# Moving a kernel's tiles by a few bytes: slots shifted by 96 bytes, and a different offset for each buffer of the weight ring

## The chip, the cores and the metric

The kernel runs on one core of a Trainium2 chip. The metric is device time of one execution in microseconds (us). Three plain executions of the kernel before took 3236.25, 3236.37 and 3238.22 us; their median is 3236.37 us.

## The reference

Two kinds of transformer block, each twice, on one sequence of 512 positions with 1024 channels, in float32. What matters here is that almost all arithmetic is products of activations with weights:

```python
for l in range(2):                       # first block
    h = rmsnorm(x, norm_mix_pre[l])
    proj = h @ w_in[l]                   # 1024 -> 7168, split into ten parts
    ...                                  # retention, two depthwise convolutions
    merged = gates0 * (ret @ w_ret_out[l]) + gates1 * (sc @ w_sc_out[l]) + gates2 * (cf @ w_cf_out[l])
    x = x + rmsnorm(merged @ w_o[l], norm_mix_post[l])
    h = rmsnorm(x, norm_ffn_pre[l])
    up = causal_dwconv(h @ w_up[l], ffn_conv_w[l])          # 1024 -> 2 * 2816
    x = x + rmsnorm((silu(gate) * val) @ w_down[l], norm_ffn_post[l])
for l in range(2):                       # second block
    proj = rmsnorm(x, pre_norm_g_2[l]) @ w_in_2[l]          # 1024 -> 10432, twelve parts
    ...                                  # gated MLP over positions, attention, a linear recurrence
    x = x + rmsnorm(merged @ w_out_2[l], post_norm_g_2[l])
```

## The kernel before

Every product is done three times over, because each float32 operand is kept as two float32r tiles, a rounded one (hi) and the rest (lo): `mm3` (lines 322, 323, 324) issues hi·hi, hi·lo and lo·hi, each with 128 rows and mostly 512 columns. A product on TensorE has a stationary operand, which a weight load brings in first, and a moving operand, which streams past it. In a row of the trace `p<-hh,whi` the name after the arrow is the moving operand and the last name the stationary one.

The operands live in four places.
- `hh` and `hl` hold the normalised activations h, transposed, hi and lo: 8 slices of 512 columns each.
- The weight ring: `wp` has seven buffers `whi` and seven `wlo`, each of 1024 columns. Weights stream from memory in pairs of pieces (`raw`, two buffers). `Stream._split` turns piece c into `whi` on ScalarE (line 179) and `wlo` on VectorE (line 180), some four pieces ahead of TensorE. Piece c lies in the buffer of c modulo 7, and there are 544 pieces.
- 48 slots `s0` to `s47` of 512 columns hold everything else: other activations (each as a hi and a lo slot when a product needs them), gates, gains. A slot that is released goes to the end of the list of free ones, and the next request takes the first of the list.
- `raw`, the small tiles and constants.

So there are three kinds of products by where the operands lie. In `projT` with h the ring is stationary and h moves (in `tok_proj` and `mla_down` the other way round). In `projT` with another operand the ring is stationary and slots move. In `out_proj` slots are stationary and the ring moves. Retention and attention multiply slots by slots.

The pools stand in a partition's memory one behind the other, in the order in which they are opened: fixed tiles, the ring, `raw`, the small tiles, the slots. Each ring buffer has 4096 bytes per partition and each slot 2048. In the built program `hh`, `hl`, all 14 ring buffers and `raw` begin 96 bytes past a multiple of 128 bytes, and all slots begin at a multiple of 128. All slices that the products take from them start a multiple of 256 bytes further on. So where h meets the ring, both operands have the same place within 128 bytes, and where a slot meets the ring, they stand 96 bytes apart.

Of the kernel before, what the change touches and what calls it, by code (L numbers as in the profile page):

```python
# [8 lines left out]
F32 = mybir.dt.float32  # L9
F32R = mybir.dt.float32r  # L10
# [13 lines left out]
RING = 7  # L24
AHEAD = 4
RAW = 2
NSLOT = 48


C_Q, C_K, C_V, C_G = 0, 256, 512, 1024  # L30
# [79 lines left out]
class Slots:  # L110
    def __init__(self, pool, n, tag):
        self.pool, self.tag = pool, tag
        self.free_ = deque(range(n))
        self.where = {}
        self.low = n
        self.cnt = 0
# [30 lines left out]
class Stream:  # L147
# [21 lines left out]
    def _split(self, c):  # L169
        nc = self.k.nc  # L170
        p = c // 2
        while self.loaded <= p:
            self._load(self.loaded)
            self.loaded += 1
        raw = self.raw[p]
        src = raw[:, 1024 * (c % 2):1024 * (c % 2) + 1024]
        hi = self.k.wp.tile([128, 1024], F32R, tag="whi", name=f"whi{c}")
        lo = self.k.wp.tile([128, 1024], F32R, tag="wlo", name=f"wlo{c}")
        nc.scalar.activation(hi[:], src, AF.Copy)  # L179
        nc.vector.tensor_tensor(lo[:], src, hi[:].bitcast(F32), op=ALU.subtract)  # L180
        self.parts[c] = (hi, lo)
        self.parts.pop(c - RING, None)

        if c % 2 == 1 and self.total is not None:
            if self.loaded < (self.total + 1) // 2 and self.loaded <= p + RAW:
                self._load(self.loaded)
                self.loaded += 1
# [50 lines left out]
class Kernel:  # L238
    def __init__(self, nc, tc, ctx, aps, total):
        self.nc, self.tc = nc, tc  # L240
        self.x_in, self.w, self.pv_in, self.rows, self.gmw, self.cst, self.out = aps
        fixed = ctx.enter_context(tc.tile_pool(name="fixed", bufs=1))
        self.wp = ctx.enter_context(tc.tile_pool(name="wp", bufs=RING))
        self.rawp = ctx.enter_context(tc.tile_pool(name="rawp", bufs=RAW))
        self.sm = ctx.enter_context(tc.tile_pool(name="small", bufs=6))
        self.s = Slots(ctx.enter_context(tc.tile_pool(name="slots", bufs=1)), NSLOT, "s")
        self.p = Slots(ctx.enter_context(tc.tile_pool(name="psum", bufs=1, space=bass.MemoryType.PSUM)), 8, "p")
        self.ws = Stream(self, total)
        self.ident = fixed.tile([128, 128], F32, tag="ident", name="ident")
        self.pv = fixed.tile([128, PV["n"]], F32, tag="pv", name="pv")  # L250
        self.half = fixed.tile([128, 4], F32, tag="half", name="half")
        self.hh = fixed.tile([128, KD, S], F32R, tag="hh", name="hh")
        self.hl = fixed.tile([128, KD, S], F32R, tag="hl", name="hl")
        self.xd = tc.dram_tile((S, D), F32, name="xd")
        self.h_op = [Op(self.hh[:, k, :], self.hl[:, k, :]) for k in range(KD)]
        self.lanes = {}
        self.x_src = self.x_in
        self.pend = None
        self.ht = {}
        self.pre = {}  # L260
        self.x = {}
# [1243 lines left out]
```

## Time and profile before

| | |
|---|---|
| median of three executions | 3236.37 us |
| profiled execution, whole time | 3238.38 us |
| its span, first to last instruction | 3236.5 us |
| TensorE busy | 3181.7 us (98%), 14808 matmuls |
| weight loads busy | 2650.7 us (82%) |
| VectorE, ScalarE, GpSimd busy | 58%, 37%, 8% |
| mean share of the 2.4 GHz TensorE clock granted | 0.994 |

The 1.9 us by which the whole time exceeds the span lie before and behind the first and last instruction. Matmuls are pipelined: the next one starts while one still shows as busy, so a matmul's duration in a row is longer than its share of the time. What a matmul costs is the step from its start to the start of the next one.

### The profile page before, as it was taken

To read this page: it belongs to the slowest core of one execution; us is meant where nothing else is said; L and a number is where in the kernel's file an instruction comes from. 1 tells how busy PE (TensorE), PEld (TensorE's weight loads), DVE (VectorE), ACT (ScalarE), POOL (GpSimd) and SP (SyncE) were. 2 spreads that over 40 slices of the span, in tenths; PEclk is the share of its full clock that TensorE was granted. 3 is DMA by queue.
4 is the path that set the end of the run, shared out by engine and by line. 5 is a ranking of instruction groups with operands and counts; after the bars stand their busy time and mean duration, and the time that the engine had idled before them with its cause. 6 is when DMAs were issued, how large, how long until landed. Compare 5 with 4: busy or idle time off the path is not lost. (4 is left out here: it accounts for less than half of the span.)

```text
span 3236.5 us, 36908 instructions
## 1 busy us (share of the span) xinstructions
PE 3181.7 (98%) x14808; PEld 2650.7 (82%) x14808; DVE 1867.2 (58%) x2729; ACT 1191.5 (37%) x1798; POOL 255.9 (8%) x362
## 2 busy tenths in 40 slices
PE   8999999999999999999999999999999999999998
PEld 7888888888888888888888887788888888778886
DVE  5687556663568755666358536635446844663643
ACT  4222343332422234333345526512234543632222
POOL 2000010000200001000010002200002001210000
PEclk9999999999999999999999999999999999999999
DMA  5222322232422232223222224322333213332221
GB/s 194 92 97 91 130 90 93 101 113 102 153 92 98 91 130 79 104 93 115 104 104 93 78 95 125 112 104 91 108 121 124 78 67 120 98 124 104 91 104 72
DMA packets 62540, 337.98 MB, mean 104 GB/s; under 512 B 10305, under 2 KB 10433, under 8 KB 27553
## 3 DMA queue, kind: packets, MB, share of 16 engines
q1 hardware_dynamic: 49984, 302.54, 26.5%
q0 software_dynamic: 11232, 31.08, 3.3%
q8 instruction: 116, 1.90, 0.2%
q10 hardware_dynamic: 1152, 2.01, 0.2%
q14 instruction: 56, 0.45, 0.0%
HBM read 310.68 MB, written 8.39 MB: 99 GB/s over the span
## 5 line engine op out<-in xcount | busy, mean ns | idle before, releaser
L322 PE MATMUL p<-hh,whi 128*128 128x512 f32 (+1 forms) x2752 | 1052.7, 383 | 1.6 <-ACT whi L179 1.6
L324 PE MATMUL p<-hh,wlo 128*128 128x512 f32 (+1 forms) x2752 | 1048.6, 381 | 1.5 <-DVE wlo L180 1.5
L323 PE MATMUL p<-hl,whi 128*128 128x512 f32 (+1 forms) x2752 | 1048.4, 381 | 0.0
L180 DVE TENSOR_TENSOR wlo<-raw,whi 128x1024 fp32r<-128x1024 f32 x544 | 675.7, 1249 | 522.0 <-ACT whi L179 520.8
L179 ACT ACTIVATE whi<-raw 128x1024 fp32r<-128x1024 f32 x544 | 562.7, 1052 | 287.8 <-PE p L324 197.6
L322 PEld LDWEIGHTS p<-hh,whi 128*128 128x128 f32 x2752 | 521.0, 189 | 99.6 <-ACT whi L179 2.0
L324 PEld LDWEIGHTS p<-hh,wlo 128*128 128x128 f32 x2752 | 520.0, 189 | 100.5 <-DVE wlo L180 1.8
L323 PEld LDWEIGHTS p<-hl,whi 128*128 128x128 f32 x2752 | 520.5, 189 | 96.8
L323 PE MATMUL p<-s,whi 128*128 128x512 f32 (+1 forms) x768 | 306.1, 399 | 2.4 <-POOL s L307 2.4
L322 PE MATMUL p<-s,whi 128*128 128x512 f32 (+1 forms) x768 | 305.9, 398 | 1.8 <-ACT s L306 1.8
L324 PE MATMUL p<-s,wlo 128*128 128x512 f32 (+1 forms) x768 | 305.7, 398 | 0.0
L323 PE MATMUL p<-wlo,s 128*128 128x512 f32 x640 | 254.1, 397 | 0.0
L322 PE MATMUL p<-whi,s 128*128 128x512 f32 x640 | 253.7, 396 | 0.0
L324 PE MATMUL p<-whi,s 128*128 128x512 f32 x640 | 252.3, 394 | 0.0
L306 ACT ACTIVATE s<-s 128x512 fp32r<-128x512 f32 x168 | 103.2, 627 | 363.6 <-DVE s L688 133.7
L672 ACT ACTIVATE s<-p 128x512 f32<-128x512 f32 x96 | 57.3, 597 | 468.6 <-PE p L324 468.6
L812 DVE SCALAR_TENSOR_TENSOR s<-p,pv,s 128x511 f32<-128x511 f32 (+1 forms) x176 | 131.8, 749 | 122.3 <-ACT s L809 119.2
L683 DVE TENSOR_TENSOR s<-p,s 128x512 f32<-128x512 f32 x96 | 66.3, 691 | 203.6 <-PE p L324 203.5
L566 DVE SCALAR_TENSOR_TENSOR s<-s,pv,s 128x511 f32<-128x511 f32 (+14 forms) x240 | 176.1, 734 | 5.7
L323 PEld LDWEIGHTS p<-s,whi 128*128 128x128 f32 (+1 forms) x768 | 145.5, 189 | 37.8 <-POOL s L307 3.9
L322 PEld LDWEIGHTS p<-s,whi 128*128 128x128 f32 (+1 forms) x768 | 145.0, 189 | 35.8 <-ACT s L306 2.7
L324 PEld LDWEIGHTS p<-s,wlo 128*128 128x128 f32 (+1 forms) x768 | 145.5, 189 | 34.5
(187 smaller groups left out, 3077.5 us busy)
## 6 DMA issues: line engine op xcount, KB each, us to landing
raw<-in_w_dram SPq DMA_DIRECT2D x272, 1024.0 KB, 4.8
s<-in_rows_dram POOLq DMA_DIRECT2D x32, 256.0 KB, 3.5
s<-s POOLq DMA_DIRECT2D x96, 64.0 KB, 2.5
xd<-s SPq DMA_DIRECT2D x24, 256.0 KB, 2.0
s<-xd POOLq DMA_DIRECT2D x24, 256.0 KB, 3.3
s<-s SPq DMA_DIRECT2D x88, 64.0 KB, 2.7
s<-in_cst_dram POOLq DMA_DIRECT2D x16, 256.0 KB, 3.8
s<-in_x_dram POOLq DMA_DIRECT2D x8, 256.0 KB, 5.8
```

The source lines that it names most:

```text
L179: nc.scalar.activation(hi[:], src, AF.Copy)
L180: nc.vector.tensor_tensor(lo[:], src, hi[:].bitcast(F32), op=ALU.subtract)
L306: self.nc.scalar.activation(hi[:, :n], t[:, :n], AF.Copy)
L322: mm(ps, a[0], b[0], start=first, stop=False)
L323: mm(ps, a[0], b[1], start=False, stop=False)
L324: mm(ps, a[1], b[0], start=False, stop=last)
L566: nc.vector.scalar_tensor_tensor(c[:, sh:], glu[:, :S - sh], w(k), c[:, sh:], op0=ALU.mult, op1=ALU.add)
L672: nc.scalar.activation(sgs[m][:], pg[:], AF.Sigmoid)
L683: nc.vector.tensor_tensor(sg[:], py[:], sg[:], op=ALU.mult)
L812: nc.vector.scalar_tensor_tensor(t[:, sh:], ps[:, :S - sh], w(k), t[:, sh:], op0=ALU.mult, op1=ALU.add)
```

## The change

```diff
-NSLOT = 48
+NSLOT = 47
+
+HI_AT = (0, 8, 16, 24, 4, 12, 20)
+LO_AT = (28, 2, 6, 10, 14, 18, 30)
...
-        hi = self.k.wp.tile([128, 1024], F32R, tag="whi", name=f"whi{c}")
-        lo = self.k.wp.tile([128, 1024], F32R, tag="wlo", name=f"wlo{c}")
+        hi = self.k.wp.tile([128, 1024 + 32], F32R, tag="whi", name=f"whi{c}")
+        lo = self.k.wp.tile([128, 1024 + 32], F32R, tag="wlo", name=f"wlo{c}")
+        ho, lo_ = HI_AT[c % RING], LO_AT[c % RING]
+        hi, lo = hi[:, ho:ho + 1024], lo[:, lo_:lo_ + 1024]
         nc.scalar.activation(hi[:], src, AF.Copy)
         nc.vector.tensor_tensor(lo[:], src, hi[:].bitcast(F32), op=ALU.subtract)
...
         self.sm = ctx.enter_context(tc.tile_pool(name="small", bufs=6))
+        self.sm.tile([128, 24], F32, tag="shift", name="shift", bufs=1)
```

A ring buffer grows from 4096 to 4224 bytes, 33 times 128, so all buffers still begin 96 bytes past a multiple of 128; the piece in it begins a further 0 to 120 bytes on. In bytes, by c modulo 7, `whi` is moved by 0, 32, 64, 96, 16, 48, 80 and `wlo` by 112, 8, 24, 40, 56, 72, 120. The tile `shift` of 96 bytes, which nothing reads or writes, stands ahead of the slots, and with it the 47 slots begin 96 bytes past a multiple of 128, as `hh` and `hl` do. The 14 times 128 bytes take the room of one slot.

So after the change h and the slots have one place within 128 bytes, and the distance from either of them to the ring is the offset of the piece. No engine's instructions are moved, added or left out: on each of the five engines the built programs have the same rows in the same order, but for the numbers of slots.

## Rows read from the trace of the kernel before

**Rows 1.** The page: span, busy time of TensorE, granted clock in 40 slices.
```profile
span 3236.5 us, 36908 instructions
PE 3181.7 (98%) x14808; PEld 2650.7 (82%) x14808; DVE 1867.2 (58%) x2729; ACT 1191.5 (37%) x1798; POOL 255.9 (8%) x362
PEclk9999999999999999999999999999999999999999
```

**Rows 2.** Matmuls by line and shape: count | busy us, mean ns | idle before, releaser.
```profile
L322 PE MATMUL p<-hh,whi 128*128 128x512 f32 x2496 | 978.1, 392 | 0.0
L324 PE MATMUL p<-hh,wlo 128*128 128x512 f32 x2496 | 974.9, 391 | 0.0
L323 PE MATMUL p<-s,whi 128*128 128x512 f32 x752 | 299.7, 399 | 2.4 <-POOL s L307 2.4
L323 PE MATMUL p<-wlo,s 128*128 128x512 f32 x640 | 254.1, 397 | 0.0
L323 PE MATMUL p<-wlo,hh 128*128 128x512 f32 x192 | 74.8, 390 | 0.0
L322 PE MATMUL p<-hh,whi 128*128 128x256 f32 x256 | 74.6, 291 | 1.6 <-ACT whi L179 1.6
L324 PE MATMUL p<-hh,wlo 128*128 128x256 f32 x256 | 73.8, 288 | 1.5 <-DVE wlo L180 1.5
L323 PE MATMUL p<-wlo,hh 128*128 128x384 f32 x64 | 23.2, 362 | 5.1 <-DVE wlo L180 5.1
L1170 PE MATMUL p<-s,whi 96*128 96x512 f32 x24 | 10.7, 446 | 10.5 <-DVE whi L1160 10.5
L323 PE MATMUL p<-s,whi 112*128 112x512 f32 x16 | 6.4, 401 | 0.0
L999 PE MATMUL p<-s,s 128*128 128x512 f32 x16 | 6.3, 397 | 0.0
L1000 PE MATMUL p<-s,s 128*128 128x512 f32 x16 | 6.3, 392 | 0.0
```

**Rows 3.** Timeline of TensorE, h moving, ring stationary: start us, us, instruction.
```profile
199.75 0.39 PE L323 MATMUL p<-hl,whi 128*128 128x512 f32 x1
...
208.59 0.39 PE L323 MATMUL p<-hl,whi 128*128 128x512 f32 x1
```

**Rows 4.** The same, halves of h (256 columns) moving.
```profile
1280.91 0.28 PE L323 MATMUL p<-hl,whi 128*128 128x256 f32 x1
...
1282.95 0.28 PE L322 MATMUL p<-hh,whi 128*128 128x256 f32 x1
```

**Rows 5.** The same, ring moving, slots stationary.
```profile
446.20 0.40 PE L322 MATMUL p<-whi,s 128*128 128x512 f32 x1
...
453.20 0.40 PE L322 MATMUL p<-whi,s 128*128 128x512 f32 x1
```

**Rows 6.** The same, slots moving, then h, the ring stationary in both.
```profile
1913.69 0.40 PE L322 MATMUL p<-s,whi 128*128 128x512 f32 x1
...
1920.02 0.39 PE L322 MATMUL p<-hh,whi 128*128 128x512 f32 x1
...
1922.11 0.39 PE L322 MATMUL p<-hh,whi 128*128 128x512 f32 x1
...
1923.92 0.39 PE L324 MATMUL p<-hh,wlo 128*128 128x512 f32 x1
```

**Rows 7.** What TensorE waited for: us in total, times, longest us.
```profile
PE p L415 <- DVE s L399: 15.6, 8, 10.9
PE p L1170 <- DVE whi L1160: 10.5, 2, 5.3
PE p L323 <- DVE wlo L180: 5.1, 4, 1.8
...
PE p L1026 <- DVE s L1015: 2.4, 2, 1.2
```

**Rows 8.** The two instructions that fill the ring.
```profile
L180 DVE TENSOR_TENSOR wlo<-raw,whi 128x1024 fp32r<-128x1024 f32 x544 | 675.7, 1249 | 522.0 <-ACT whi L179 520.8
L179 ACT ACTIVATE whi<-raw 128x1024 fp32r<-128x1024 f32 x544 | 562.7, 1052 | 287.8 <-PE p L324 197.6 <-DMA raw<-in_w_dram 67.4 <-DVE wlo L180 9.1
```

## The prediction

> **What bounds the kernel now.** I read the page first: TensorE is busy for 98% of the span and its clock is granted in full in all 40 slices [rows 1]. Then the list of its waits: the three longest kinds come to 31 us of 3236, and those for the ring's two fillers are a few us [rows 7]. So nothing feeds TensorE late; the kernel takes as long as its matmuls stand one behind the other. The next question is what one matmul costs, as the step from start to start, and that is read from timelines.
>
> Where h meets the ring, 39 steps of 512-column matmuls take 208.59 - 199.75 = 8.84 us, 226.7 ns each [rows 3]. Halves of 256 columns take (1282.95 - 1280.91) / 17 = 120.0 ns [rows 4]. The 256 further columns thus cost 106.7 ns, 0.417 ns each, which is one column per period of 2.4 GHz. So 512 columns are 213.3 ns, and each matmul carries 13.3 ns on top.
>
> Where a slot meets the ring, the same matmul costs more: 7.00 us for 30 steps, 233.3 ns, with the ring moving and slots stationary [rows 5]; 6.33 us for 27, 234.4 ns, with slots moving and the ring stationary [rows 6]. The groups by shape show that this holds over the span: mean durations of 390 to 392 ns with h against 397 to 399 with slots, in either role [rows 2]. Shape, lines and clock are the same; what differs is where the operands lie. With h both stand at the same place within 128 bytes, with a slot they are 96 bytes apart. That is no proof: slots are another region too, and they are written by more engines. One stretch helps. When h takes over from slots, the first 9 steps still take 2.09 us, 232.2 ns each, and only then do 8 steps take 1.81 us, 226 ns [rows 6]. So an equal place does not give the short step at once; a run of like matmuls settles into it. And slot against slot, at equal places (both at 0) but in chains of a few matmuls, shows 392 and 397 ns [rows 2], like unsettled ones.
>
> **The change part by part.** The matmuls that it touches are counted from the groups. With h: 3 x 2496 + 3 x 192 = 8064 of 512 columns, now at 226.7 ns. With slots against the ring: 3 x 752 + 3 x 640 = 4176, and 72 more of the recurrence's gates (3 x 16 of 112 rows and 24 of 96), 4248, now at 233.9 ns (the mean of 233.3 and 234.4 by their counts). Both kinds will meet the ring under the same conditions, since h and slots come to one place; call their common step x. The time changes by 8064 (x - 226.7) + 4248 (x - 233.9) ns, which is nothing at x = 229.2 ns.
>
> What is x? The step is set by the moving operand of one matmul and the weights that are loaded beside it for the next one. Two of three loads with a stationary ring are `whi`, one is `wlo`. Of the seven `whi` places one has offset 0, as h has now: between 226.7 ns settled and 232.2 unsettled, I take 229.5. Two have 32 and 96 bytes, which are the two distances (96 bytes in one direction or the other, counted within 128) that slots have now: 233.9 ns. The other four, and all `wlo`, have distances that the trace does not show. Their bounds are the nearest rows on either side, 226.7 and 233.9; between them I take the middle, 230.3. Below 226.7 no settled stretch goes, though 213.3 ns of columns is the floor. Then x = 2/3 (229.5 + 2 x 233.9 + 4 x 230.3) / 7 + 1/3 x 230.3 = 2/3 x 231.2 + 76.8 = 230.9 ns. With h that is +4.2 ns x 8064 = +33.9 us, with slots -3.0 ns x 4248 = -12.7 us, together +21 us.
>
> The Trainium skill speaks against counting anything here ("SBUF — State Buffer", section "Who interferes with whom"): TensorE has two independent read ports, one for the moving operand and one for weight loads, and never waits on anyone. By it the step would not depend on places and the sum would be nothing. The trace doesn't bear that out as it stands: equal shapes differ by 7 ns.
>
> The 256-column matmuls (768), the 384- and 320-column ones (384) and slot against slot: the first have 13.3 ns on top as the long ones do, and by the same 4.2 ns could add up to 5 us; slot against slot keeps equal places. I put 2 us down for the lot. The ring's fillers: 1052 and 1249 ns for a piece [rows 8], each once in 3236 / 544 = 5.9 us, four pieces ahead. Written at other offsets they may get longer, but VectorE is busy for 58% and a tenth more on 1249 ns stays within the idle time ahead of it (522 us in all, for the ring's other filler). If that cover were gone, TensorE's waits for the two, now 8 us [rows 2, 7], would grow; I put nothing. One slot fewer: the free list of 48 was down to one left at 4 of 1538 requests, all in attention; with 47 it is empty there, and 14 requests find one or none behind them. Each then waits for the last reader of a slot just released, and behind it wait the split or copy on that engine and the scores' matmuls. TensorE's longest kind of wait in attention is 2.4 us now [rows 7]; between nothing and some 5 us, I take 1.
>
> Sum: 21 + 2 + 1 = +24 us on 3238.4 us, the profiled execution's own time, which is 2 us above the median of the runs. On the median that gives 3236.4 + 24 = 3260 us.
>
> **The rivals.**
> *All steps as bad as slots now.* If any distance but 0 gives 233.9 ns, and pieces change too often to settle, x = 233.9: 8064 x 7.2 = +58 us, 3294 us. For it: only distance 0, in long runs, shows the short step. Against it: only two other distances are known.
>
> *The other side: faster.* If settling needs only that distances stay put within a piece (24 matmuls with one pair of buffers), and slots lose what made them slow, x = 226.7: -7.2 x 4248 = -31 us, 3206 us. It decides from x below 229.2 ns on. For it: an unsettled stretch lasts 9 steps and a piece has 24. Against it: with slots, whose distance is the same in every matmul, long stretches never settle [rows 5, 6].
>
> *No change.* If the 7 ns belong to the slots' region and not to the place within 128 bytes, x stays at either value, 3236 us. For it: slot against slot is slow at equal places. Against it: the unsettled stretch has h alone and is nearly as slow, 232.2 ns.
>
> *Far faster.* If distances exist at which a load and a stream don't meet at all, the 13.3 and 20 ns on top shrink. Halving both would give -6.7 x 8064 - 10.3 x 4248 = -98 us, 3139 us. No row shows any such step. The Trainium skill has a rule for it ("TensorE: Matmul & The Clock Gate", section "Back-to-back issue gap"): a warm matmul's gap is N / 2.4 + 2.5 ns, 216 ns at 512 columns; by it, as an estimate, the kernel would come to 3236 - 8064 x 0.0107 - 4248 x 0.0179 = 3074 us. The trace shows 226.7 at best.
>
> **How the numbers follow.** A measurement of this kernel can tell about 0.2%, 6.5 us, from no change. Mixed steps, x from 229.8 to 232.8 (+8 to +45 us): 0.45; the forecast, 3260 us, with a range of its own of 3244 to 3281. All bad, beyond +45: 0.14. No change within 6.5 us, by place or by balance: 0.13. Settled steps, faster by up to 45 us: 0.24. Far faster: 0.04. So faster 0.28, same 0.13, slower 0.59. The range reaches from the settled case, 3206, to just under the worst, 3292.
>
> **What would show it.** In the groups by shape the 512-column durations with h should rise from 391 to about 395 ns, and those with slots should fall from 398 to about the same. Timelines should show steps that differ from piece to piece with a period of seven pieces: shortest where c modulo 7 is 0, some 234 ns at 1 and 3. TensorE's waits, the fillers' means and attention should stay as they are. The prediction is wrong if h keeps 391 ns, if slots keep 398, or if the new distances give steps under 226 ns.

## The result, and the profile after

The changed kernel takes 3256.34 us (median of three executions, 3253.68 to 3256.89) against 3236.37 us: 1.0062 times as long, with a 95% interval of 1.0044 to 1.008. It is slower by 20 us, where 24 were forecast. The profiled execution took 3256.89 us, with a span of 3254.8 us.

The matmuls of the changed kernel by line and shape, with the same columns as [rows 2] (lines 322 to 324 have become 328 to 330):

```profile
L328 PE MATMUL p<-hh,whi 128*128 128x512 f32 x2496 | 985.3, 395 | 0.0
L330 PE MATMUL p<-hh,wlo 128*128 128x512 f32 x2496 | 983.3, 394 | 0.0
...
L329 PE MATMUL p<-s,whi 128*128 128x512 f32 x752 | 296.5, 394 | 1.7 <-POOL s L313 1.7
...
L329 PE MATMUL p<-wlo,s 128*128 128x512 f32 x640 | 251.9, 394 | 0.0
...
L329 PE MATMUL p<-wlo,hh 128*128 128x512 f32 x192 | 75.7, 394 | 0.0
...
L328 PE MATMUL p<-hh,whi 128*128 128x256 f32 x256 | 74.1, 290 | 1.6 <-ACT whi L184 1.6
```

Matmuls with h went from 390 to 392 ns up to 393 to 395, those with slots from 394 to 399 down to 394 and 395. The two kinds have met, as forecast. The short ones of 256 columns stayed (290 against 291).

The timeline of TensorE, first the stretch of [rows 3], h against the ring; then one of slots against the ring, which answers to [rows 6]:

```profile
199.39 0.40 PE L329 MATMUL p<-hl,whi 128*128 128x512 f32 x1
...
202.63 0.39 PE L328 MATMUL p<-hh,whi 128*128 128x512 f32 x1
...
206.06 0.39 PE L328 MATMUL p<-hh,whi 128*128 128x512 f32 x1
...
208.85 0.39 PE L328 MATMUL p<-hh,whi 128*128 128x512 f32 x1
...
1924.45 0.40 PE L328 MATMUL p<-s,whi 128*128 128x512 f32 x1
...
1931.38 0.39 PE L328 MATMUL p<-s,whi 128*128 128x512 f32 x1
...
1934.79 0.39 PE L328 MATMUL p<-s,whi 128*128 128x512 f32 x1
```

With h, 41 steps take 9.46 us, 230.7 ns each, and they differ on the way: 15 of 228.7 ns (202.63 to 206.06), then 12 of 232.5. With slots, 30 steps of 231.0 ns are followed by 15 of 227.3. So the step now depends on the piece and no more on what meets it. Over all steps of at most 250 ns between two 512-column matmuls against the ring, the trace of before has a mean of 227.0 ns with h (7859 steps) and 233.6 with slots (4063), that of after 231.1 and 231.4.

TensorE's waits: the longest kinds, us in total, times, longest us; they answer to [rows 7]:

```profile
PE p L421 <- DVE s L405: 16.9, 11, 11.0
PE p L1176 <- DVE whi L1166: 8.2, 2, 4.1
PE p L329 <- DVE wlo L185: 5.4, 4, 1.8
```

And the ring's fillers, which answer to [rows 8]:

```profile
L185 DVE TENSOR_TENSOR wlo<-raw,whi 128x1024 fp32r<-128x1024 f32 x544 | 676.3, 1251 | 529.8 <-ACT whi L184 528.9
L184 ACT ACTIVATE whi<-raw 128x1024 fp32r<-128x1024 f32 x544 | 562.6, 1052 | 292.9 <-PE p L330 200.4 <-DMA raw<-in_w_dram 68.2 <-PE p L329 14.8
```

Both fillers take as long as before, 1251 and 1052 ns; writing at the new offsets costs them nothing that shows.

### The profile page after: what moved, and what is told of

Its sections match the earlier page's. It is cut to its first block, busy times and chain, and to the rows that moved or that the text cites. A ratio compares the mean times of both kernels' runs of the same rounds, so it can differ in the third digit from the quotient of the medians.

```text
span 3254.8 us, 36944 instructions
## 1 busy us (share of the span) xinstructions
PE 3200.5 (98%) x14808; PEld 2646.7 (81%) x14808; DVE 1866.4 (57%) x2729; ACT 1191.9 (37%) x1798; POOL 257.6 (8%) x362
## 5 line engine op out<-in xcount | busy, mean ns | idle before, releaser
L185 DVE TENSOR_TENSOR wlo<-raw,whi 128x1024 fp32r<-128x1024 f32 x544 | 676.3, 1251 | 529.8 <-ACT whi L184 528.9
L184 ACT ACTIVATE whi<-raw 128x1024 fp32r<-128x1024 f32 x544 | 562.6, 1052 | 292.9 <-PE p L330 200.4
```

## The experiments

**First: is it the distance?** Three kernels have the form of the changed one, with one offset for all 14 buffers. The fourth is the kernel before with one slot fewer.

`k0`, all offsets 0:
```diff
-HI_AT = (0, 8, 16, 24, 4, 12, 20)
-LO_AT = (28, 2, 6, 10, 14, 18, 30)
+HI_AT = (0,) * 7
+LO_AT = (0,) * 7
```


> The changed kernel with all 14 offsets at 0 (47 slots, slots shifted): h, slots and ring all stand at one place within 128 bytes. Distance theory (the step is set by the distance of moving operand and loaded weights within 128 bytes): slots against the ring fall from 233.9 to 226.7 ns as with h, 4248 x -7.2 = -31 us, 3206 us (up to 3211 with one slot fewer). Region theory (slots are slow because of where they lie or who writes them): slots stay at 234 ns, h at 226.7, 3236 us.

`k32` and `k64`, the same with 8 and 16 in place of 0:

> The changed kernel with all 14 offsets at 32 bytes: one distance everywhere, 32 bytes, the size of the one that slots had before with the ring stationary. Distance theory: all steps at about 233.9 ns, with h too: 8064 x 7.2 = +58 us, 3294 us. Settling theory (any constant distance settles, only changes of distance cost): h stays at 226.7, slots fall to it, 3206 us. Region theory: h 226.7, slots 234, 3236 us.

> The changed kernel with all 14 offsets at 64 bytes. Distance theory with a period of 64 bytes: as with 0, 3206 to 3211 us, steps of 226.7 ns throughout. Distance theory with a period of 128 bytes: somewhere between 226.7 and 233.9 ns or above, 3215 to 3294 us. Settling theory: 3206 us. Region theory: 3236 us.

`n47`:
```diff
-NSLOT = 48
+NSLOT = 47
```


> The kernel before with 47 slots and nothing else changed. The prediction's estimate for one slot fewer is +1 us between bounds of 0 and 5: 3236 to 3241 us, steps as before. A rival is that other slot numbers alone move the time by more than that.

Measured, each against the kernel before on the same chip:

| | median us | ratio | interval |
|---|---|---|---|
| k0 | 3263.85 | 1.0090 | 1.0075 to 1.0105 |
| k32 | 3273.93 | 1.0121 | 1.0106 to 1.0136 |
| k64 | 3257.37 | 1.0071 | 1.0054 to 1.0088 |
| n47 | 3234.77 | 1.0001 | 0.9992 to 1.0011 |

The loss of a slot costs nothing that shows. `k0` misses both times that were named for it (3206 and 3236 us) and `k32` all three of its own (3294, 3206 and 3236); `k64` lies in the wide band that was given for a period of 128 bytes, 3215 to 3294 us. With every offset at 0 the kernel is slower than with the 14 different ones, and h, which stands 0 from the ring within 128 bytes as it did before, has lost its short step. Its groups:

```profile
L330 PE MATMUL p<-hh,wlo 128*128 128x512 f32 x2496 | 992.3, 398 | 0.0
L329 PE MATMUL p<-hl,whi 128*128 128x512 f32 x2496 | 989.0, 396 | 0.0
L328 PE MATMUL p<-hh,whi 128*128 128x512 f32 x2496 | 981.9, 393 | 0.0
...
L330 PE MATMUL p<-s,wlo 128*128 128x512 f32 x752 | 299.1, 398 | 0.0
L329 PE MATMUL p<-s,whi 128*128 128x512 f32 x752 | 298.2, 397 | 1.7 <-POOL s L313 1.7
L328 PE MATMUL p<-s,whi 128*128 128x512 f32 x752 | 295.6, 393 | 0.8 <-ACT s L312 0.8
```

h and slots have the same durations line by line (393, 396 or 397, 398), so the region theory is out: what counts is the distance from the ring. But the distance within 128 bytes is not enough to tell it. What else changed for h between the kernel before and `k0` is the size of the ring's buffers: 4096 bytes is 16 times 256, while 4224 is 16.5 times 256, so that neighbouring buffers now stand 128 bytes apart within 256. The addresses in the built program, set beside the trace of `k0`, give for each step the distance from the moving operand to the weights loaded beside it, which are those of the next matmul. Taken within 512 bytes, the steps with h moving in which `whi` is in place and `whi` is loaded next come out at 226.9 ns at 0, 233.4 at 128, 227.0 at 256 and 233.3 at 384: 0 goes with 256, and 128 with 384. But the steps from lines 329 and 330 are long at either distance, 232 to 235 ns. Hence a new theory: the period is 256 bytes, and `whi` and `wlo` must both be right.

**Second: a period of 256 bytes.** `s96` is the kernel before with the shift of the slots alone. In it h, ring and slots all stand 224 past a multiple of 256, and slots and ring are 256 apart within 512.
```diff
+        self.sm.tile([128, 24], F32, tag="shift", name="shift", bufs=1)
         self.s = Slots(ctx.enter_context(tc.tile_pool(name="slots", bufs=1)), NSLOT, "s")
```


> The kernel before with the slots shifted by 96 bytes and nothing else: ring buffers of 4096 bytes and 48 slots stay. h and ring stand 0 apart within 512 bytes as before, slots and ring 256 apart. Theory of 256 bytes (the step is short when the moving operand and the loaded weights, whi and wlo alike, stand at one place within 256 bytes): slots fall from 233.9 to 226.7 ns, 3236 - 31 = 3205 us. Theory of 512 bytes (one place within 512): slots stay at 231 to 234 ns, 3224 to 3236 us. Region theory: 3236 us.

`t256`, `t128` and `tlo` have the form of the changed kernel with its 4224-byte buffers. But buffers and pieces are tied, since in the changed kernel they are not quite: from piece 337 on, and again from piece 467 on, the numbers are off by one buffer more, so that an offset that belongs to c modulo 7 doesn't always meet the same buffer. Tied, `whi` and `wlo` take turns in memory, 128 bytes apart within 256.
```diff
-HI_AT = (0, 8, 16, 24, 4, 12, 20)
-LO_AT = (28, 2, 6, 10, 14, 18, 30)
+HI_AT = (0,) * 7
+LO_AT = (32,) * 7
...
-        hi = self.k.wp.tile([128, 1024 + 32], F32R, tag="whi", name=f"whi{c}")
-        lo = self.k.wp.tile([128, 1024 + 32], F32R, tag="wlo", name=f"wlo{c}")
+        hi = self.k.wp.tile([128, 1024 + 32], F32R, tag=f"whi{c % RING}", name=f"whi{c}", bufs=1)
+        lo = self.k.wp.tile([128, 1024 + 32], F32R, tag=f"wlo{c % RING}", name=f"wlo{c}", bufs=1)
```


> The changed kernel with each ring buffer tied to c modulo 7 and its places laid so that whi (offset 0) and wlo (offset 128) stand at one place with h and slots within 256 bytes, at 0 or 256 within 512; buffers of 4224 bytes and 47 slots stay. Theory of 256: steps of 226.7 ns throughout, 3205 us. Theory of 512: half of the pieces at the wrong place, x about 230, 3250 us. If the buffers' size itself were what costs: as with all offsets at 0, 3264 us.

`t128` has the two offsets exchanged, `tlo` has both at 0:

> The same with whi at offset 128 and wlo at 0, so that all ring pieces stand 128 bytes from h and slots within 256, and whi and wlo at one place with each other. Theory of 256: loads at 128 bytes had steps of 233 to 235 ns where all offsets were 0; x about 233, 8064 x 6.3 - 4248 x 0.9 = +47 us, 3283 us. Rival (only the distance from whi to wlo counts, not that to the moving operand): 226.7 ns, 3205 us.

> The same with both offsets 0: whi at one place with h and slots within 256 bytes, wlo 128 bytes off. Theory of 256: as pieces of c modulo 7 = 0 were where all offsets were 0, steps of 228, 232 and 234 ns on the three lines, x about 231.6, +39 - 10 us, 3265 us. Rival (a stretch settles if two of three loads are at the right place): 3210 us.

| | places within 256 | median us | ratio | interval |
|---|---|---|---|---|
| s96 | all at one | 3207.97 | 0.9913 | 0.9896 to 0.9929 |
| t256 | all at one | 3217.87 | 0.9945 | 0.9930 to 0.9960 |
| t128 | ring 128 off | 3279.64 | 1.0133 | 1.0118 to 1.0148 |
| tlo | wlo alone 128 off | 3258.28 | 1.0064 | 1.0049 to 1.0079 |

The theory of 256 called the order of all four, and the times of `s96`, `t128` and `tlo` within 7 us (3205, 3283 and 3265 were expected); `t256` is 13 us longer than it said, and the last batch deals with that. The timeline of `s96`, the ring moving and slots stationary, which answers to [rows 5], shows 44 steps in 9.98 us, 226.8 ns each, where there were 233.3:

```profile
440.43 0.39 PE L323 MATMUL p<-whi,s 128*128 128x512 f32 x1
...
450.41 0.39 PE L325 MATMUL p<-whi,s 128*128 128x512 f32 x1
```

Its groups are level at 389 to 392 ns, with slots as with h:

```profile
L323 PE MATMUL p<-hh,whi 128*128 128x512 f32 x2496 | 976.0, 391 | 0.0
...
L324 PE MATMUL p<-s,whi 128*128 128x512 f32 x752 | 294.5, 392 | 2.5 <-POOL s L308 2.5
...
L324 PE MATMUL p<-wlo,s 128*128 128x512 f32 x640 | 249.1, 389 | 0.0
```

In `t128`, h against the ring, 39 steps take 9.10 us, 233.3 ns each:

```profile
199.31 0.39 PE L328 MATMUL p<-hh,whi 128*128 128x512 f32 x1
...
208.41 0.40 PE L328 MATMUL p<-hh,whi 128*128 128x512 f32 x1
```

`tlo` shows where the misplaced load is paid. Its groups:

```profile
L330 PE MATMUL p<-hh,wlo 128*128 128x512 f32 x2496 | 991.9, 397 | 1.6 <-DVE wlo L185 1.6
L329 PE MATMUL p<-hl,whi 128*128 128x512 f32 x2496 | 989.5, 396 | 0.0
L328 PE MATMUL p<-hh,whi 128*128 128x512 f32 x2496 | 976.1, 391 | 0.0
```

One load of three is out of place, that of `wlo` for line 330, which goes on beside line 329. Line 328 keeps 391 ns, line 329 has 396, and line 330 has 397, although the weights loaded beside it are in place again. So one misplaced load lengthens two steps, the one that it goes on beside and the one behind. Over 39 steps of h against the ring the mean is 9.01 / 39 = 231.0 ns:

```profile
199.34 0.40 PE L329 MATMUL p<-hl,whi 128*128 128x512 f32 x1
...
208.35 0.40 PE L329 MATMUL p<-hl,whi 128*128 128x512 f32 x1
```

Where the ring moves, `tlo` has one moving operand of three out of place, and only its own line is long:

```profile
L329 PE MATMUL p<-wlo,s 128*128 128x512 f32 x640 | 252.7, 395 | 0.0
L328 PE MATMUL p<-whi,s 128*128 128x512 f32 x640 | 250.6, 392 | 0.0
L330 PE MATMUL p<-whi,s 128*128 128x512 f32 x640 | 248.8, 389 | 0.0
```

The rival that two right loads in three would do is out.

**Third: does the place itself count, do smaller distances do better, and where do the 10 us of t256 come from?** All four start from `s96`. `all0` moves `hh` and all that stands behind it:
```diff
+        fixed.tile([128, 8], F32, tag="pad", name="pad")
         self.hh = fixed.tile([128, KD, S], F32R, tag="hh", name="hh")
```


> Slots shifted by 96 bytes as in the run s96, and h, ring, raw and all behind them moved by 32 bytes more, so that h and ring stand at 0 within 256 bytes and slots too. Theory of 256 (only the distance counts): as s96, 3208 us, steps of 226.8 ns. Rival (the place itself counts as well, 96 bytes past a multiple of 128 being a good one): longer or shorter by some us per ns of step, 12.3 us for each ns.

`d32` moves the ring alone (the slots are held where they were); `d64` the same by 64 bytes:
```diff
+        self.wp.tile([128, 8], F32, tag="ahead", name="ahead", bufs=1)
         self.rawp = ctx.enter_context(tc.tile_pool(name="rawp", bufs=RAW))
...
-        self.sm.tile([128, 24], F32, tag="shift", name="shift", bufs=1)
+        self.sm.tile([128, 16], F32, tag="shift", name="shift", bufs=1)
```


> The run s96 with the ring (buffers of 4096 bytes) moved by 32 bytes against h and slots: one distance of 32 everywhere. Theory of 256, by the mixed run with all offsets at 32 (232 to 234 ns): x about 233, 8064 x 6.3 - 4248 x 0.9 = +47 us on before, 3283 us. Rival (a small distance still settles): 3208 us.

> The same with 64 bytes. By the mixed run with all offsets at 64 (229 to 235 ns, the loads at 64 themselves 229 to 231): x about 230.5, 8064 x 3.8 - 4248 x 3.4 = +16 us on before, 3252 us. If 64 were as good as 0: 3208 us; as bad as 128: 3280 us.

`tied` takes from `t256` the tags alone:
```diff
-        hi = self.k.wp.tile([128, 1024], F32R, tag="whi", name=f"whi{c}")
-        lo = self.k.wp.tile([128, 1024], F32R, tag="wlo", name=f"wlo{c}")
+        hi = self.k.wp.tile([128, 1024], F32R, tag=f"whi{c % RING}", name=f"whi{c}", bufs=1)
+        lo = self.k.wp.tile([128, 1024], F32R, tag=f"wlo{c % RING}", name=f"wlo{c}", bufs=1)
```


> The run s96 with each ring buffer tied to c modulo 7, as the run t256 had it. If the 10 us by which t256 was longer than s96 come from the tying (a buffer that is still in use holds up the next piece, and TensorE waits longer for pieces): 3218 us. If they come from the larger buffers or from one slot fewer, now that steps are short: 3208 us.

| | median us | ratio | interval |
|---|---|---|---|
| all0 | 3210.41 | 0.9917 | 0.9902 to 0.9932 |
| d32 | 3276.00 | 1.0125 | 1.0108 to 1.0142 |
| d64 | 3266.17 | 1.0090 | 1.0075 to 1.0105 |
| tied | 3220.94 | 0.9951 | 0.9936 to 0.9966 |

`all0` and `s96` agree within their intervals: at the one other place that was tried, only the distance counts. A distance of 32 bytes, constant everywhere, costs as much as one of 128: in `d32` 39 steps of h against the ring take 9.10 us again, 233.3 ns each, and nothing settles at a shorter step:

```profile
199.42 0.40 PE L325 MATMUL p<-hl,whi 128*128 128x512 f32 x1
...
208.52 0.40 PE L325 MATMUL p<-hl,whi 128*128 128x512 f32 x1
```

`d64` missed its expectation by 14 us. With h or slots moving and the ring 64 bytes ahead it is as bad as the others, 395 to 397 ns; with the ring moving, so that the loaded weights are 64 bytes behind, 392 and 393:

```profile
L325 PE MATMUL p<-hl,whi 128*128 128x512 f32 x2496 | 986.8, 395 | 0.0
...
L325 PE MATMUL p<-s,whi 128*128 128x512 f32 x752 | 297.8, 396 | 1.8 <-POOL s L309 1.8
...
L325 PE MATMUL p<-wlo,s 128*128 128x512 f32 x640 | 251.6, 393 | 0.0
L324 PE MATMUL p<-whi,s 128*128 128x512 f32 x640 | 251.2, 392 | 0.0
```

In `d64` the direction and the role of the ring change together. In `k64`, whose buffers stand by turns at 64 and 192 bytes, both directions occur with the ring stationary: the steps of its trace have a mean of 233.0 ns with the load 64 bytes ahead of the moving operand and 230.7 with it 64 behind. So the direction seems to count, though in `k64` each step can also carry something of the one ahead of it, as in `tlo`.

`tied` is 13 us longer than `s96` with steps as short (226.9 ns with h in both), so the 10 us of `t256` are the price of tying buffers to c modulo 7. Half of it shows in TensorE's waits, 53.7 us in all against 47.7: that of line 1171 is 14.9 us against 10.5, and that of line 325 has grown from 1.5 us, once, to 3.0. Another 4 us are TensorE's clock, which stands at its lower level for longer, and the two add up to most of the 12 us by which the spans differ.

```profile
PE p L1171 <- DVE whi L1161: 14.9, 4, 5.2
...
PE p L325 <- DVE wlo L180: 3.0, 3, 1.5
```

## Why the prediction was right, point by point

**What bounds the kernel, and what a matmul costs.** Right in the main. The times above follow the steps, but for those of `tied` and `t256`, and TensorE's waits come to 43.3 us before and 43.0 after. The clock was read too favourably: a digit 9 of [rows 1] stands for 90% or more and doesn't say that the clock is granted in full.

**x = 230.9 ns, +33.9 us with h and -12.7 with slots.** The trace of after has 231.1 ns with h and 231.4 with slots, where that of before has 227.0 and 233.6. By the forecast's counts that is 8064 x 4.1 = +33 us and 4248 x -2.2 = -9 us, +24 together, against the forecast's +21. The spans differ by 18.3 us only. Most of the rest is a term that the forecast doesn't have, TensorE's clock. In the trace of before it stands at the lower of its two levels, 1.2 GHz, in six stretches ahead of the last matmul, 34 us together; in that of after in five, 20 us. One of them, before: a wait, then matmuls at the lower level, and the granted clock of the seven microseconds, the last number but two (0.51):

```profile
2023.03 0.80 PE L1170 MATMUL p<-s,whi 96*128 96x512 f32 x1 [5.12 <-DVE whi L1160]
2023.62 0.63 PE L322 MATMUL p<-s,whi 128*128 128x512 f32 x1
2024.05 0.63 PE L323 MATMUL p<-s,whi 128*128 128x512 f32 x1
...
2021.00:2028.00 7.00, 4.97 (x12) 3.96 (x13) 4.05 (x6) 3.10 (x4) 1.28 (x1) 0.51 0.49 169
```

A step of 512 columns is 0.43 us there. Counted as what starts in such stretches stand further apart than their columns at 2.4 GHz and 20 ns, for those over 30 ns, the lower clock costs 13 us before and 9 after, while the gaps outside of them stay at 79 and 80 us.

**The step behind x.** Here the reason was incomplete, and the number came out partly by luck. The prediction took the place within 128 bytes for what counts, put the piece with offset 0 between a settled and an unsettled step, and put all unseen distances halfway. The runs fit a period of 256 bytes: 256 apart is as good as 0 (`s96`), 128 apart is not (`t128`). Since the change makes the buffers 16.5 x 256 bytes long, it moves every other buffer by 128 bytes before any offset is applied, which is a distance that costs 6 ns (`t128`). So the change has a part that the prediction didn't see at all: with the shift and the larger buffers and no offsets (`k0`) the kernel takes 3264 us, 56 us more than with the shift alone (`s96`). The 14 offsets then make it better, not worse: 3256 us. They spread the distances within 256 bytes, and by the steps of the traces the spread is cheaper in the mean (231.1 ns with h) than having one of `whi` and `wlo` at 0 and the other at 128 in each piece (232.2 in `k0`). The middle value for unseen distances stood in well for that mixture, and piece by piece one sees the luck. With two thirds of `whi` and one of `wlo`, the forecast's terms are 229.8 ns for a piece with c modulo 7 = 0, 232.7 for 1 and 3, and 230.3 for the four others. The trace, over the pieces up to 336 with h moving, has 227.1 ns at 0, 232.7 and 231.9 at 1 and 3, and 230.1, 232.5, 231.1 and 231.3 at 2, 4, 5 and 6. Misses from -2.7 to +2.2 ns cancel: the means of the seven are 230.9 and 231.0.

**The rivals.** That h settles and slots lose what makes them slow, 3206 us, is what the shift does alone (`s96`, 3208 us): this rival had the right step for slots, and the larger buffers kept it from happening. But its condition, that distances need only stay put, is wrong: in `d32` they stay put, and all steps are long. They have to be right. That all is as bad as slots, 3294 us, has its like in `d32` (3276) and `t128` (3280): uniformly wrong distances cost some 233 ns rather than 233.9. No change by region is refuted by `s96`, in which the slots' region is as fast as any other. Far faster steps were not found: in all runs the groups of 512 columns with h or slots against the ring have mean steps from 226 ns up, but for one of 225.7 in `tlo` (line 330, the ring moving and h stationary), right behind a long one. The gap of some 216 ns that the Trainium skill gives for a matmul by itself ("TensorE: Matmul & The Clock Gate", section "Back-to-back issue gap") is not reached by these float32r matmuls with a weight load each. By the Trainium skill TensorE's two read ports are independent and it waits on no one ("SBUF — State Buffer", section "Who interferes with whom"). The runs show that the step depends on where the two operands stand to each other: `s96` and `d32` differ by 32 bytes in the ring's place and by 68 us. Whether that arises at the ports, no run shows.

**One slot fewer, the fillers, the short matmuls.** Taken at 1, 0 and 2 us; `n47` measures no difference (0.9992 to 1.0011), the fillers kept their means, and the 256-column groups did not lengthen.

**The signs.** Durations did rise from 391 to 395 and fall from 398 to 394. The pattern with a period of seven pieces came too, up to piece 336: shortest at 0 and long at 1 and 3, as forecast, but 4 (232.5 ns) is as long, and the pieces of one remainder differ from each other by 0.5 ns or less (standard deviation).

What stays open is why the period is 256 bytes and what exactly meets what in the memory; the runs show the distance, its direction and the price, not the mechanism. Distances of 8 to 24 bytes were not tried by themselves. The changed kernel's trace has a hint: in its pieces with c modulo 7 = 0, up to 336, `whi` stands at 0 and `wlo` 16 bytes behind h within 256, and their steps are 227.1 ns all the same. `s96`, 0.9913 of the kernel before, beats both kernels.

## What to carry to other kernels

Where TensorE is the bound and nothing feeds it late, read the step from start to start by operand region, and if equal shapes differ by a few ns, look at the places of the operands in memory early. Here the moving operand and the weights loaded beside it should start at the same place within 256 bytes; padding that changes a buffer's length by anything but a multiple of 256 undoes that for the buffers behind it, unless their offsets make up for it (`t256`). Spreading buffers over different offsets was not a cure: one common place won by 48 us over fourteen different ones.

## What the runs showed of the hardware that was not expected

- Equal matmuls of 128x512 float32r cost 226.9 ns in the mean with h where moving operand and loaded weights stand 0 apart within 256 bytes (`s96`), 233.3 ns at a constant distance of 32 (`d32`) and 232.6 at 128 (`t128`).
- One misplaced weight load in three lengthens two steps out of three: 231.0 ns in the mean over 39 steps of `tlo`, with only the step ahead of both still short. One misplaced moving operand in three lengthens its own line alone (395 ns against 392 and 389).
- A distance of 64 bytes cost more with the ring stationary and ahead (395 to 397 ns) than with the ring moving and the loaded weights behind (392 and 393).
- After a stretch with a wrong distance, matmuls at the right one took nine steps to settle [rows 6]. That is the longest case: of eight such take-overs at the full clock in the trace of before, two took nine steps and the others two to five.
